# A hybrid layer's MLP on one core: the down projection by Strassen's seven products, interleaved with the next block's up products

## The chip, the core and the metric

The kernel runs on one core of one Trainium2 chip. TensorE (PE) multiplies matrices, VectorE (DVE), ScalarE (ACT) and GpSimd (POOL) work element by element, and SyncE (SP), POOL and others issue DMA transfers. The metric is the device time of one launch in microseconds (us).

## The reference, cut to what matters

One layer is computed for 384 tokens of 2048 features, all in float32: 256 tokens of a new stream ("prompt") and 128 of running streams ("sample"). A mixer comes first (one wide input projection, a pooling branch, a state-space scan, an output projection), then the part that is changed, the MLP:

```
x = x + rmsnorm(m, g_mix_post)
hdn = square(relu(rmsnorm(x, g_mlp_pre) @ w_up)) @ w_down      # 2048 -> 8192 -> 2048
x = x + rmsnorm(hdn, g_mlp_post)
```

## The kernel before, in words

**Three passes for one product.** Every float32 operand of a large product is split in two: `h` is the value rounded to the type fp32r (an ACT copy), `l` the rest (a DVE subtraction). A product is then three matmuls of 128 x 128 by a moving operand: h by h, h by l, l by h, summed in PSUM (`mm3`, L79; `half`, L84, makes 24 of them from half of a weight tile). `wfetch` (L61) has SP load 128 x 1024 weights (512 KB), `wsplit` (L66) splits them. Weights as loaded, `h` and `l` have three buffers each.

**Stages.** Tokens lie in three blocks of 128 (`b` = 0 and 1 prompt, 2 sample). In the input projection (`proj`, L93; 129 tiles of 128 outputs: 16 pool, 16 + 16 gates, 1 dt, 80 for scan and z), in the gate, pool, scan and up projections the weights are the stationary operand and 384 tokens the moving one: one tile of 128 outputs over 2048 inputs is 48 matmuls of 384 columns. The tokens' halves are `xgh`/`xgl` for the input projection, `ah`/`al` (`A`) for the pool projection, `abh`/`abl` for the scan's, `x1h`/`x1l` (`xs2`, L717 to L727) for the up projection. In the output and down projections (`moving`, L641) the tokens are stationary (`mh`/`ml`, `hh`/`hl`) and 512 columns of weights move.

**The MLP** (L730 on) goes over 8 blocks (`c8`) of 1024 of the 8192 hidden features. For each block it makes eight up tiles: 48 matmuls, then DVE's relu with the norm (L763), ACT's square (L764), the split to `hh`/`hl` (L767, L768). Then it takes the down products in four groups of 512 columns (`nb`), each 8 x 3 x 3 = 72 matmuls of 512 columns. `done` (L773) adds them to `hacc` in SBUF on DVE (L778; a copy by ACT in the first block, L776). In the last block each column group is squared, summed and multiplied with `g_mlp_post`, and the last one is followed by the norm (`postnorm`), the residual `x1` and the output. `x1` stays in SBUF throughout.

**Order.** The order on each engine is set by the tile framework's planner from the order of the program, with a few held back by hand (`hold`, `gate`). Tiles lie in pools at addresses that follow from the pools' order and sizes; small `pad` tiles (L212, L634) only move what comes after them.

Of the kernel before, what the change touches and what calls it, by code (L numbers as in the profile page):

```python
# [34 lines left out]
def build(ctx, tc, io):  # L35
# [8 lines left out]

    cst = consts.tile([P, C_END], F32, name="cst")
    vec = consts.tile([P, V_END], F32, name="vec")
# [3 lines left out]
    def mmtile(name):  # L50
        return psm.tile([P, 512], F32, tag="mm", name=name)
# [24 lines left out]
    def wload(src, name):  # L76
        return wsplit(wfetch(src, name))
# [133 lines left out]

    small.tile([P, 24], F32, name="pad_small")  # L212
    tok = small.tile([P, 11, NH], F32, name="tok")
    decb = small.tile([P, NH, NB], F32, name="decb")
    with tc.tile_pool(name="phc", bufs=1, reuse_waits="tile") as pc, tc.tile_pool(name="phc2", bufs=2, reuse_waits="tile") as pc2:
# [10 lines left out]
        def pool_tile(gi, k4):  # L226
# [35 lines left out]
            )  # L262
            rc = cst[:, C_RC + gi * 16 : C_RC + gi * 16 + 16]
            v.tensor_tensor(d[:, :16], cur[:, 15:31], rc, ALU.mult)
# [33 lines left out]
        def dt_phase(pb):  # L298
# [22 lines left out]
            v.tensor_scalar(dta, dt, nA, -1.0, ALU.mult, ALU.mult)  # L321
            v.tensor_tensor_scan(cum, cst[:NH, C_SCAN : C_SCAN + T], dta, 0.0, ALU.mult, ALU.add)
            sy.dma_start(cum_scr, cum)
# [45 lines left out]
    with tc.tile_pool(name="phd", bufs=2, reuse_waits="tile") as pd, tc.tile_pool(  # L369
# [46 lines left out]
        for g in range(G):  # L416
# [27 lines left out]
            for p4 in range(4):  # L444
# [8 lines left out]
                CT[:, TP:].unsqueeze(1).to_broadcast([P, 2, P]),  # L453
                cst[:, C_CM : C_CM + 256].rearrange("p (a t) -> p a t", a=2),
                ALU.mult,
# [6 lines left out]
            cbm = pd.tile([P, 512], F32, tag="cbm", name=f"cbm{g}")  # L462
            v.tensor_tensor(cbm, cb, cst[:, C_MASK : C_MASK + 512], ALU.mult)

# [170 lines left out]

    res = ctx.enter_context(tc.tile_pool(name="res", bufs=1, reuse_waits="tile"))

    x1 = res.tile([P, 3, DM], F32, name="x1")
    r2 = res.tile([P, T], F32, name="r2")

    def moving(o, units, lhs, tail, done):  # L641
# [41 lines left out]
    with tc.tile_pool(name="phf", bufs=1, side="right", reuse_waits="tile") as pf, tc.tile_pool(  # L683
# [19 lines left out]
        for i in range(4):  # L703
# [10 lines left out]
            if i == 0:  # L714
                gate[1] = ins
    pga = ctx.enter_context(tc.tile_pool(name="pga", bufs=1, reuse_waits="tile"))
    xs2 = []  # L717
    for k in range(KD):
# [8 lines left out]
        xs2.append((h, l))  # L727
    mpool.close()

    with tc.tile_pool(name="phg", bufs=1, reuse_waits="tile") as pg, tc.tile_pool(  # L730
        name="phg2", bufs=2, reuse_waits="tile"
    ) as pg2:
        st = pg.tile([P, 3, 4], F32, name="st2")
        for b in range(3):
            for i in range(4):
                q = pg2.tile([P, 512], F32, tag="q3", name=f"q2_{b}_{i}")
                s.activation(q, x1[:, b, blk(i)], AF.Square, accum_out=st[:, b, i : i + 1])
        dg = pg.tile([P, 3, P], F32, name="dg2")
        for b in range(3):
            y = postnorm(pg2, st, b, "n2")  # L740
# [4 lines left out]
        hacc = pg.tile([P, 3, DM], F32, name="hacc")  # L745
        gpo = pg.tile([P, DM], F32, name="gpo2")
        gp.dma_start(gpo, io["g_mlp_post"].partition_broadcast(P))
        st3 = pg.tile([P, 3, 4], F32, name="st3")
        NC = 8
        for c8 in range(NC):  # L750
            hh = []
            for f8 in range(8):
                f = c8 * 8 + f8
                if f == 0:
                    ps = mmtile("pj_up0")[:, :T]
                    half(ps, 0, wload(io["w_up"][0, 0], "up0_0"), xs2)
                    hold[:] = gate
                    half(ps, 1, wload(io["w_up"][0, 1], "up0_1"), xs2)
                else:
                    ps = proj([io["w_up"][f, 0], io["w_up"][f, 1]], xs2, f"up{f}")  # L760
                    hold[:] = [None, None]
                t = pg2.tile([P, T], F32, tag="t", name=f"ht{f}")
                v.scalar_tensor_tensor(out=t, in0=ps, scalar=0.0, in1=r2, op0=ALU.max, op1=ALU.mult)  # L763
                s.activation(t, t, AF.Square)  # L764
                h = pg2.tile([P, T], F32R, tag=f"hh{f8}", name=f"hh{f}", bufs=1)
                l = pg2.tile([P, T], F32R, tag=f"hl{f8}", name=f"hl{f}", bufs=1)
                s.activation(h, t, AF.Copy)  # L767
                v.tensor_tensor(l, t, h.bitcast(F32), ALU.subtract)  # L768
                hh.append((h, l))
            for nb in range(4):  # L770
                o = [mmtile(f"wd{c8}_{nb}_{b}") for b in range(3)]

                def done(b):  # L773
                    dst = hacc[:, b, blk(nb)]
                    if c8 == 0:
                        s.copy(dst, o[b])  # L776
                        return
                    v.tensor_tensor(dst, o[b], dst, ALU.add)  # L778
                    if c8 < NC - 1:
                        return  # L780
                    q = pg2.tile([P, 512], F32, tag="q3", name=f"q3_{nb}_{b}")
                    s.activation(q, dst, AF.Square, accum_out=st3[:, b, nb : nb + 1])
                    v.tensor_tensor(dst, dst, gpo[:, blk(nb)], ALU.mult)
                    if nb < 3:
                        return
                    y = postnorm(pg2, st3, b, "n3")
                    for i in range(4):
                        z = hacc[:, b, blk(i)]
                        xb = x1[:, b, blk(i)]
                        if i >= (0, 2, 3)[b]:  # L790
                            s.activation(z, z, AF.Copy, scale=y)
                            gp.tensor_tensor(z, z, xb, ALU.add)
                        else:
                            v.scalar_tensor_tensor(out=z, in0=z, scalar=y, in1=xb, op0=ALU.mult, op1=ALU.add)
                        sy.dma_start(io["y"][b][:, blk(i)], z)

                moving(
                    o,
                    [(io["w_down"][c8, nb, kp], f"wd{c8}_{nb}_{kp}") for kp in range(4)],
                    hh,  # L800
                    3 if c8 == NC - 1 and nb == 3 else 0,
                    done,
                )


# [30 lines left out]
def _moving(np, w):  # L836
    r, c = w.shape
    return np.ascontiguousarray(w.reshape(r // 256, 2, P, c // 512, 512).transpose(3, 0, 2, 1, 4)).reshape(c // 512, r // 256, P, 1024)


# [79 lines left out]
```

## Time and profile before

| What | us |
|---|---|
| Time of a launch, median of 3 runs (2887.78 to 2889.4) | 2888.16 |
| Span of the profiled execution, first to last instruction | 2886.1 |
| PE busy | 2862.9 (99%) |
| DVE busy | 1548.9 (54%) |
| ACT busy | 1108.4 (38%) |
| POOL busy | 142.4 (5%) |
| Bytes read from and written to HBM | 404.48 and 41.72 MB |

The profile is one execution. Its page gives each engine's busy time, the same in 40 equal slices of the span (a digit is tenths), the DMA queues, the chain of work that ended last followed back from the last instruction, and groups of equal instructions: line, engine, operation, output and inputs, shapes, count, then busy us, mean ns of one, and the idle time before them with what ended it. The trace behind it can be asked for single instructions in order of time: start (us), duration (us), engine, line, operation, tiles. Matmuls overlap one another in these records, so what one costs is read from the distance between starts. Line numbers are those of the kernel before.

### The profile page before, as it was taken

The page shows a single profiled execution, that of the slowest core. Times are in us where ns is not written, and L with a number is a line of the kernel's source. Part 1 is how long each engine was busy: PE and PEld are TensorE (multiplying, and loading weights), DVE is VectorE, ACT ScalarE, POOL GpSimd, SP SyncE. Part 2 cuts the span into 40 slices and gives each one's busy share as a digit, 9 for nine tenths or more (in the row PEclk, how much of TensorE's full clock was granted, in tenths as well). Part 3 has the DMA queues.
Part 4 walks back from the last instruction along what each step waited for, and adds up shares of the span by engine and source line. Part 5 has one row for each costly group of instructions (what it writes and reads, how often), then busy time and mean ns, then how long its engine had stood idle before and what let it go on. Part 6 is the DMA issues. An engine that isn't in the chain of part 4 may idle for free.

```text
span 2886.1 us, 40192 instructions
## 1 busy us (share of the span) xinstructions
PE 2862.9 (99%) x16165; PEld 2702.5 (94%) x16165; DVE 1548.9 (54%) x2306; ACT 1108.4 (38%) x1628; POOL 142.4 (5%) x178
## 2 busy tenths in 40 slices
PE   9999999999999999999999999999999999999998
PEld 8999999999999999999999988989898998989896
DVE  7773335668678678677533334534444444444445
ACT  5343224445445345344422223533232333333233
POOL 0000000011011011011000000000000000000001
PEclk9999999999999999999999999999999999999999
DMA  6444445466456456466744453434443444444443
GB/s 214 132 130 140 137 137 190 149 200 211 160 196 211 151 203 210 146 221 204 224 147 152 146 179 120 130 126 130 126 130 126 130 126 131 125 131 124 131 125 117
DMA packets 141914, 448.82 MB, mean 156 GB/s; under 512 B 17456, under 2 KB 41072, under 8 KB 137120
## 3 DMA queue, kind: packets, MB, share of 16 engines
q1 hardware_dynamic: 133152, 410.14, 44.9%
q0 software_dynamic: 8576, 36.13, 3.3%
q8 instruction: 126, 2.06, 0.3%
q14 instruction: 60, 0.49, 0.1%
HBM read 404.48 MB, written 41.72 MB: 155 GB/s over the span
## 4 chain that ended last, share of the span: by engine, by line
PE 98%; DVE 1%; DMA 0%; ACT 0%; issue 0%; SPq 0%; DVEq 0%; ACTq 0%
PE pj_up L82 6%; PE pj_up L81 6%; PE pj_up L80 6%; PE wd L650 6%; PE wd L649 6%; PE wd L648 6%; PE pj_x L82 5%; PE pj_x L80 5%; PE pj_x L81 5%; PE pj_z L81 3%; PE pj_z L82 3%; PE pj_z L80 3%; PE pj_sp L80 3%; PE pj_sp L82 3%; PE pj_sp L81 3%; PE pj_gb L80 2%
## 5 line engine op out<-in xcount | busy, mean ns | idle before, releaser
L81 PE MATMUL pj_up<-x1l,wh_up 128*128 128x384 f32 x1024 | 343.2, 335 | 0.0
L80 PE MATMUL pj_up<-x1h,wh_up 128*128 128x384 f32 x1024 | 343.1, 335 | 0.0
L82 PE MATMUL pj_up<-x1h,wl_up 128*128 128x384 f32 x1024 | 342.7, 335 | 0.0
L650 PE MATMUL wd<-wh_wd,hl 128*128 128x512 f32 x768 | 298.9, 389 | 0.0
L649 PE MATMUL wd<-wl_wd,hh 128*128 128x512 f32 x768 | 298.9, 389 | 0.0
L648 PE MATMUL wd<-wh_wd,hh 128*128 128x512 f32 x768 | 298.7, 389 | 0.0
L73 DVE TENSOR_TENSOR wl_wd<-w_wd,wh_wd 128x1024 fp32r<-128x1024 f32 x128 | 156.9, 1225 | 263.2 <-ACT wh_wd L71 263.2
L71 ACT ACTIVATE wh_wd<-w_wd 128x1024 fp32r<-128x1024 f32 x128 | 136.1, 1063 | 350.9 <-PE wd L650 284.3
L80 PE MATMUL pj_x<-xgh,wh_x 128*128 128x384 f32 x768 | 264.0, 344 | 0.0
L73 DVE TENSOR_TENSOR wl_up<-w_up,wh_up 128x1024 fp32r<-128x1024 f32 x128 | 156.9, 1226 | 198.1 <-ACT wh_up L71 198.1
L82 PE MATMUL pj_x<-xgh,wl_x 128*128 128x384 f32 x768 | 261.0, 340 | 0.0
L71 ACT ACTIVATE wh_up<-w_up 128x1024 fp32r<-128x1024 f32 x128 | 135.9, 1064 | 325.6 <-PE pj_up L81 264.8
L81 PE MATMUL pj_x<-xgl,wh_x 128*128 128x384 f32 x768 | 259.8, 338 | 0.0
L80 PEld LDWEIGHTS pj_up<-x1h,wh_up 128*128 128x128 f32 x1024 | 192.5, 188 | 0.7 <-ACT x1h L725 0.4
L81 PEld LDWEIGHTS pj_up<-x1l,wh_up 128*128 128x128 f32 x1024 | 192.6, 188 | 0.4
L82 PEld LDWEIGHTS pj_up<-x1h,wl_up 128*128 128x128 f32 x1024 | 192.5, 188 | 0.1
L81 PE MATMUL pj_z<-xgl,wh_z 128*128 128x384 f32 x512 | 173.1, 338 | 0.0
L80 PE MATMUL pj_z<-xgh,wh_z 128*128 128x384 f32 x512 | 172.9, 338 | 0.0
L82 PE MATMUL pj_z<-xgh,wl_z 128*128 128x384 f32 x512 | 172.9, 338 | 0.0
L650 PEld LDWEIGHTS wd<-wh_wd,hl 128*128 128x128 f32 x768 | 144.1, 188 | 30.0
L649 PEld LDWEIGHTS wd<-wl_wd,hh 128*128 128x128 f32 x768 | 144.1, 188 | 29.9
L648 PEld LDWEIGHTS wd<-wh_wd,hh 128*128 128x128 f32 x768 | 144.2, 188 | 29.6
(280 smaller groups left out, 6230.9 us busy)
## 6 DMA issues: line engine op xcount, KB each, us to landing
w_up<-w_up SPq DMA_DIRECT2D x128, 512.0 KB, 3.4
w_wd<-w_down SPq DMA_DIRECT2D x128, 512.0 KB, 3.4
w_x<-w_in SPq DMA_DIRECT2D x96, 512.0 KB, 3.7
w_z<-w_in SPq DMA_DIRECT2D x64, 512.0 KB, 3.5
w_sp<-w_ssd SPq DMA_DIRECT2D x64, 512.0 KB, 3.5
w_ga<-w_in SPq DMA_DIRECT2D x32, 512.0 KB, 3.5
w_pp<-w_pp SPq DMA_DIRECT2D x32, 512.0 KB, 3.5
hs<-ssm SPq DMA_DIRECT2D x16, 1024.0 KB, 6.3
```

Source lines behind the costliest of these rows:

```text
L71: s.activation(h, w, AF.Copy)
L73: v.tensor_tensor(l, w, h.bitcast(F32), ALU.subtract)
L80: te.matmul(out, wh, xh, start=first, stop=False)
L81: te.matmul(out, wh, xl, start=False, stop=False)
L82: return te.matmul(out, wl, xh, start=False, stop=last)
L648: te.matmul(o[b], mh, wh[:, c], start=k == 0, stop=False)
L649: te.matmul(o[b], mh, wl[:, c], start=False, stop=False)
L650: te.matmul(o[b], ml, wh[:, c], start=False, stop=k == nk - 1)
```

## The change

**Seven products.** For the first seven blocks the down product of the 256 prompt tokens is made by the Winograd form of Strassen's scheme. The 1024 features are cut in two halves of 512, 1024 columns at a time (`p` = 0, 1) in two of 512, and the tokens in two of 128. The seven products are made from blocks of tokens, blocks of weights, four sums of token blocks (`token_sums`: five additions and a split, in two calls for each feature block) and four sums of weight blocks (`down_units`: `add`, DVE, 2048 columns each, in place in the loaded weights `raw`). The 128 sample tokens (sums 7 and 8) are multiplied directly with the four unsummed weight blocks. `steps` lists eight weight matrices in order, each with the one or two products that it feeds and the sum that is made after its split. All eight are split, so that a feature block has 32 splits of down weights instead of 16.

**Sums over the blocks in DRAM.** Each of the nine results of a half leaves PSUM by an ACT copy to one of two buffers `ev` and a POOL transfer to `acc_scr`, plain in the first block, accumulating (`accum_op`) in the others. In the last block, whose down product is made as before, the 18 sums are loaded back (`begin_last`), seven of each half are put together by DVE (`merge`), and the last block's products are added.

**Interleaving.** A list of units is worked through by `run` in an order written out (`manual_schedule`): two halves of down weights, one half of an up tile of the next block, and so on. A unit is fetched eight units ahead and split four units ahead, after the matmuls of the unit that held the buffers; every fourth split goes to a fourth pair of buffers (`split4`). The hidden activations have two sets of buffers.

**Room and places.** `x1` goes to DRAM after the output projection and comes back in the last block; `x1h`/`x1l` move to the other side of SBUF, where `mh`/`ml` were. Most of the constants (`cst2`) move to the pool `small`, `pad_small` grows, `pad_m` goes. This moves other tiles too: counted in bytes past a multiple of 512 in the allocation of the built programs, `xgh`/`xgl` go from 128 to 0, `mh`/`ml` from 384 to 480, `x1h`/`x1l` from 0 to 480; the weight buffers and `hh`/`hl` stay at 0, `ah`/`al` at 64.

```diff
-    cst = consts.tile([P, C_END], F32, name="cst")
+    cst = consts.tile([P, 352], F32, name="cst")
...
+    cst2 = small.tile([P, C_END - C_MASK], F32, name="cst2")
...
-    sy.dma_start(cst, io["cst"])
+    sy.dma_start(cst[:, :C_MASK], io["cst"][:, :C_MASK])
+    sy.dma_start(cst2, io["cst"][:, C_MASK:])
...
-    small.tile([P, 24], F32, name="pad_small")
+    small.tile([P, 88], F32, name="pad_small")
...
-        mp.tile([P, 24], F32, name="pad_m")
...
+    x1_scr = dram.tile([P, 3, DM], F32, name="x1_scr")
+    acc_scr = [[dram.tile([P, 512], F32, name=f"acc_scr{p}_{i}") for i in range(9)] for p in range(2)]
...
-    pga = ctx.enter_context(tc.tile_pool(name="pga", bufs=1, reuse_waits="tile"))
+    gp.dma_start(x1_scr, x1)
+    mpool.close()
+    pga_hold = ExitStack()
+    pga = pga_hold.enter_context(tc.tile_pool(name="pga", bufs=1, side="right", reuse_waits="tile"))
...
+    t8 = pg.tile([P, 8, T], F32, name="t8")
+    sf = pg.tile([P, 4, 2, P], F32, name="sf")
+    sh = pg.tile([P, 4, 4, P], F32R, name="sh")
+    sl = pg.tile([P, 4, 4, P], F32R, name="sl")
...
+    DEPTH = 4
+
+    def split4(w, name):
+        turn[0] += 1
+        if turn[0] % DEPTH:
+            return wsplit((w, name))
+        h = pg.tile([P, 1024], F32R, tag="xh", name=f"wh_{name}")
+        l = pg.tile([P, 1024], F32R, tag="xl", name=f"wl_{name}")
+        s.activation(h, w, AF.Copy)
+        v.tensor_tensor(l, w, h.bitcast(F32), ALU.subtract)
+        return h, l
+
+    def run(units, far=8):
+        n = len(units)
+        got, hl = [None] * n, [None] * n
+
+        def fetch(i):
+            if i < n and units[i][0]:
+                got[i] = units[i][0]()
+
+        def prep(i):
+            if i < n:
+                hl[i] = units[i][1](got[i])
+
+        for i in range(far):
+            fetch(i)
+        for i in range(DEPTH):
+            prep(i)
+        for i, (_, _, mm, post, soon) in enumerate(units):
+            fetch(i + far)
+            mm(hl[i])
+            if soon:
+                post()
+            prep(i + DEPTH)
+            if not soon:
+                post()
+            hl[i] = got[i] = None
+
+    nothing = lambda *_: None
+
+    def token_sums(k):
+        a11, a12 = t8[:, k, :P], t8[:, 4 + k.start : 4 + k.stop, :P]
+        a21, a22 = t8[:, k, P:TP], t8[:, 4 + k.start : 4 + k.stop, P:TP]
+        f = [sf[:, i, :, :] for i in range(4)]
+        v.tensor_tensor(f[0], a22, a21, ALU.subtract)
+        v.tensor_tensor(f[3], a11, a12, ALU.subtract)
+        v.tensor_tensor(f[3], f[3], f[0], ALU.add)
+        v.tensor_tensor(f[2], a11, a21, ALU.subtract)
+        v.scalar_tensor_tensor(out=f[1], in0=f[0], scalar=-1.0, in1=a11, op0=ALU.mult, op1=ALU.subtract)
+        s.activation(sh[:, :, k, :], sf, AF.Copy)
+        v.tensor_tensor(sl[:, :, k, :], sf, sh[:, :, k, :].bitcast(F32), ALU.subtract)
+
+    def up_evict(f, ps):
+        f8 = f % 8
+        t = t8[:, f8, :]
+        v.scalar_tensor_tensor(out=t, in0=ps, scalar=0.0, in1=r2, op0=ALU.max, op1=ALU.mult)
+        s.activation(t, t, AF.Square)
+        blocks = range(3) if f8 >= 4 else (0, 2)
+        n = len(blocks)
+        tag = f"{f8}_{f // 8 % 2}"
+        h = pg.tile([P, n, P], F32R, tag=f"hh{tag}", name=f"hh{f}")
+        l = pg.tile([P, n, P], F32R, tag=f"hl{tag}", name=f"hl{f}")
+        tb = t.rearrange("p (b t) -> p b t", b=3)
+        if n == 2:
+            tb = tb[:, 0:3:2, :]
+        s.activation(h, tb, AF.Copy)
+        v.tensor_tensor(l, tb, h.bitcast(F32), ALU.subtract)
+        return {b: (h[:, i, :], l[:, i, :]) for i, b in enumerate(blocks)}
+
...
+    NAMES = ("11", "12", "22", "21")
+
+    def down_units(c8, p, hh):
+        nm = f"{c8}_{p}"
+        tok = lambda k0, b: lambda k: hh[k0 + k][b]
+        sums = lambda i: lambda k: [sh[:, i, k, :], sl[:, i, k, :]]
+        raw, t2 = {}, []
+        src = {n: io["w_down"][c8, p, i] for i, n in enumerate(NAMES)}
+
+        def add(d, n):
+            v.tensor_tensor(raw[d], raw[d], raw[n], ALU.add)
+
+        steps = [
+            ("11", True, [(0, tok(0, 0)), (7, tok(0, 2))], nothing),
+            ("12", True, [(8, tok(0, 2))], lambda: add("11", "12")),
+            ("21", True, [(1, tok(4, 0)), (7, tok(4, 2))], nothing),
+            ("22", True, [(2, sums(3)), (8, tok(4, 2))], lambda: add("12", "22")),
+            ("11", False, [(4, sums(0))], lambda: add("22", "11")),
+            ("12", False, [(6, sums(2))], lambda: add("21", "22")),
+            ("22", False, [(5, sums(1))], nothing),
+            ("21", False, [(3, tok(4, 1))], nothing),
+        ]
+        begins, ends = {7: 0, 8: 1}, {7: 2, 8: 3}
+
+        def evict(r, o):
+            e = pg.tile([P, 512], F32, tag="ev", name=f"ev{nm}_{r}", bufs=2)
+            s.copy(e, o)
+            if c8 == 0:
+                gp.dma_start(acc_scr[p][r], e)
+            else:
+                gp.dma_start(acc_scr[p][r], e, accum_op=ALU.add)
+
+        out = []
+        for j, (kd, load, uses, then) in enumerate(steps):
+            outs = []
+            for q in range(2):
+                half_cols = slice(q * 1024, q * 1024 + 1024)
+
+                def fetch(kd=kd, q=q, hc=half_cols):
+                    if q == 0:
+                        raw[kd] = pr.tile([P, 2048], F32, tag="raw", name=f"raw{nm}_{kd}")
+                    sy.dma_start(raw[kd][:, hc], src[kd][:, hc])
+
+                def prep(_, j=j, q=q, kd=kd, hc=half_cols, then=then):
+                    hl = split4(raw[kd][:, hc], f"wd{nm}_{j}_{q}")
+                    if q:
+                        then()
+                    return hl
+
+                def mm(hl, j=j, q=q, uses=uses, outs=outs):
+                    if j == 0 and q == 0:
+                        t2.extend(sstile(f"t2_{nm}_{i}") for i in range(2))
+                    if q == 0:
+                        outs += [t2[r - 7] if r >= 7 else mmtile(f"wd{nm}_{r}") for r, _ in uses]
+                    wh, wl = hl
+                    for k2 in range(2):
+                        k = q * 2 + k2
+                        c = slice(k2 * 512, k2 * 512 + 512)
+                        for (r, a), o in zip(uses, outs):
+                            ah, al = a(k)
+                            first = k == 0 and (r < 7 or begins[r] == j)
+                            fin = k == 3 and (r < 7 or ends[r] == j)
+                            te.matmul(o, ah, wh[:, c], start=first, stop=False)
+                            te.matmul(o, ah, wl[:, c], start=False, stop=False)
+                            te.matmul(o, al, wh[:, c], start=False, stop=fin)
+
+                def post(j=j, q=q, uses=uses, outs=outs):
+                    if q == 0:
+                        return
+                    for (r, _), o in zip(uses, outs):
+                        if r < 7 or ends[r] == j:
+                            evict(r, o)
+                    if p == 0 and j < 2:
+                        token_sums(slice(2 * j, 2 * j + 2))
+
+                out.append((fetch if load else None, prep, mm, post, False))
+        return out
+
...
+    def begin_last():
+        raws.close()
+        fin = ctx.enter_context(tc.tile_pool(name="fin", bufs=1, reuse_waits="tile"))
+        for p in range(2):
+            ac.append([fin.tile([P, 512], F32, name=f"ac{p}_{i}") for i in range(9)])
+            for i in range(9):
+                gp.dma_start(ac[p][i], acc_scr[p][i])
+
...
+    def enter_last():
+        pga_hold.close()
+        begin_last()
...
+        gp.dma_start(tail["gpo"], io["g_mlp_post"].partition_broadcast(P))
+        gp.dma_start(tail["x1"], x1_scr)
...
+    for i in range(NC - 1):
+        down = down_units(i, 0, hs_[i]) + down_units(i, 1, hs_[i])
+        ups = up_units(i + 1, hs_[i + 1])
+        for j in range(16):
+            units += down[2 * j : 2 * j + 2] + ups[j : j + 1]
+    last = last_units(hs_[c8])
...
+    with tc.manual_schedule():
+        run(units)
```

More of the change, by code (lines that the diff above doesn't have):

```diff
@@ L744, in build @@
         s.copy(r2, bc[:, :T])
[L745 to L758, printed above, removed]
-                else:
[L760 to L776, printed above, removed]
-                        return
[L778 to L802, printed above, removed]
-                )
@@ new lines, in up_units, with mm, post @@
+    def up_units(c8, hh, skip=0):
+        out = []
+        for f8 in range(skip, 8):
+            f = c8 * 8 + f8
+            ps = []
+            for q in range(2):
+                def mm(hl, f=f, q=q, ps=ps):
+                    if q == 0:
+                        ps.append(mmtile(f"pj_up{f}")[:, :T])
+                    half(ps[0], q, hl, xs2)
+                def post(f=f, f8=f8, q=q, ps=ps):
+                    if q:
+                        hh.append(up_evict(f, ps[0]))
+                out.append(
+                    (lambda f=f, q=q: wfetch(io["w_up"][f, q], f"up{f}_{q}"), lambda w: split4(*w), mm, post, True)
+                )
+        return out
@@ new lines, in last_done @@
+    def last_done(nb, bs, o):
+        lp2, st3, gpo = tail["lp2"], tail["st3"], tail["gpo"]
+        for b in bs:
+            v.tensor_tensor(hacc[b][nb], o[b], hacc[b][nb], ALU.add)
+        for b in bs:
+            q = lp2.tile([P, 512], F32, tag="q3", name=f"q3_{nb}_{b}")
+            s.activation(q, hacc[b][nb], AF.Square, accum_out=st3[:, b, nb : nb + 1])
+        for b in bs:
+            v.tensor_tensor(hacc[b][nb], hacc[b][nb], gpo[:, blk(nb)], ALU.mult)
+        if nb < 3:
+            return
+        for b in bs:
+            y = postnorm(lp2, st3, b, "n3")
+            for i in range(4):
+                z = hacc[b][i]
+                xb = tail["x1"][:, b, blk(i)]
+                if i >= (0, 2, 3)[b]:
+                    s.activation(z, z, AF.Copy, scale=y)
+                    gp.tensor_tensor(z, z, xb, ALU.add)
+                else:
+                    v.scalar_tensor_tensor(out=z, in0=z, scalar=y, in1=xb, op0=ALU.mult, op1=ALU.add)
+                sy.dma_start(io["y"][b][:, blk(i)], z)
@@ new lines, in build @@
+    hh0 = []
+    ps = mmtile("pj_up0")[:, :T]
+    half(ps, 0, wload(io["w_up"][0, 0], "up0_0"), xs2)
+    hold[:] = gate
+    half(ps, 1, wload(io["w_up"][0, 1], "up0_1"), xs2)
+    hold[:] = [None, None]
+    hh0.append(up_evict(0, ps))
+    hs_ = [hh0] + [[] for _ in range(NC - 1)]
+    units = up_units(0, hs_[0], 1)
+    for i in range(NC - 1):
[3 more added lines that the diff above has]
+            units += down[2 * j : 2 * j + 2] + ups[j : j + 1]
@@ L877 @@
         "w_up": _tiles(np, a["w_up"][0], range(0, 4 * DM, P)),
[L878 to L880 removed]
+        "w_down": _paired(np, a["w_down"][0][: 7 * 1024]),
+        "w_dlast": _moving(np, a["w_down"][0][7 * 1024 :]),
         "state_pool": np.ascontiguousarray(a["state_pool"][0].reshape(NB, 15, KD, P).transpose(3, 2, 0, 1)),
```

111 lines of the change are left out of this document (95 added, 16 removed).

## The prediction

> **What bounds the kernel now.** I read the page's head and chain first (which engine is the bound), then starts of single matmuls (what one costs, stage by stage), then the groups by line and the transfers (whether the other engines can carry the new work).
>
> ```profile
> span 2886.1 us, 40192 instructions
> PE 2862.9 (99%) x16165; PEld 2702.5 (94%) x16165; DVE 1548.9 (54%) x2306; ACT 1108.4 (38%) x1628; POOL 142.4 (5%) x178
> ...
> DVE  7773335668678678677533334534444444444445
> ...
> PEclk9999999999999999999999999999999999999999
> ...
> GB/s 214 132 130 140 137 137 190 149 200 211 160 196 211 151 203 210 146 221 204 224 147 152 146 179 120 130 126 130 126 130 126 130 126 131 125 131 124 131 125 117
> ...
> PE 98%; DVE 1%; DMA 0%; ACT 0%; issue 0%; SPq 0%; DVEq 0%; ACTq 0%
> ```
>
> PE is 98% of the chain that ends last, at full clock in every slice: time is number of matmuls times the step from one to the next. That step is not the "mean ns" of a group, since matmuls overlap; it is read from starts. In the MLP, by order of time:
>
> ```profile
> 1948.86 0.33 PE L80 MATMUL pj_up<-x1h,wh_up 128*128 128x384 f32 x1
> ...
> 2015.44 0.39 PE L648 MATMUL wd<-wh_wd,hh 128*128 128x512 f32 x1
> ...
> 2080.76 0.33 PE L80 MATMUL pj_up<-x1h,wh_up 128*128 128x384 f32 x1
> ```
>
> One block of 1024 features is 384 up matmuls in 66.58 us (173.4 ns each) and 288 down matmuls in 65.32 us (226.8 ns each), without a gap.
>
> The span is one profiled execution; the median of the runs, 2888.16, stands 2.1 above it, and I carry that over: forecast = 2888.2 plus the sum.
>
> **Part 1, fewer matmuls.** For each of seven blocks and each 1024 columns, the seven products of 256 prompt tokens need 7 x 4 x 3 = 84 matmuls and the 128 sample tokens 2 x 8 x 3 = 48: 132 in place of 144. Over 14 such pairs that is 168 matmuls fewer, which is also the difference of the two PE instruction lists. They are of the same form, with operands that both start at multiples of 512 bytes as before: 168 x 0.2268 = **-38.1 us**, all on the path.
>
> **Part 2, where the operands lie.** In the allocation of the built programs, counted in bytes past a multiple of 512, the weight buffers are at 0 in both kernels. The layer's input xgh/xgl goes from 128 to 0, mh/ml of the output projection from 384 to 480, x1h/x1l of the up projection from 0 to 480; ah/al stay at 64. Does it matter? The gate and pool projections alternate, same lines, same shapes:
>
> ```profile
> 299.72 0.34 PE L80 MATMUL pj_pp<-ah,wh_pp 128*128 128x384 f32 x1
> ...
> 308.04 0.33 PE L80 MATMUL pj_ga<-xgh,wh_ga 128*128 128x384 f32 x1
> ...
> 316.47 0.34 PE L80 MATMUL pj_pp<-ah,wh_pp 128*128 128x384 f32 x1
> ...
> 324.79 0.33 PE L80 MATMUL pj_ga<-xgh,wh_ga 128*128 128x384 f32 x1
> ...
> L648 PE MATMUL wo<-wh_wo,mh x192: 390/393/404, 1669.5 to 1802.6; 128*128 128x512 f32 x192
> ```
>
> 48 matmuls on ah (at 64) take 8.32 us, both times; 48 on xgh (at 128) take 8.43; 48 up matmuls (at 0) took 66.58/8 = 8.32. The output projection steps (1802.6 - 1669.5)/573 = 232.3 ns, the down projection 226.8, at the same width: the first has its operands 384 bytes apart, the second 0. So distances 0 and 64 go with the short step, 128 and 384 with the long. The 129 projections of the layer's input lie at distance 0 afterwards: 129 x 0.11 = **-14.2 us**. The instruction order up to the MLP is otherwise the same, row for row. The output projection's weights lie 32 bytes beyond its tokens afterwards, between the two fast distances: 576 x 5.5 ns = **-3.2 us** (0 if not). The up projection's moving operand gets 480, that is 32 short of 512; nothing in the trace has that distance. The nearest row is distance 0, so I take no cost; like distance 128 it would be 64 x 0.11 = +7.0 us.
>
> [...]
>
> **Part 3, the new work of DVE and ACT beside PE.**
>
> ```profile
> 1948.90:2080.80 131.90, 131.90 (x674) 120.63 (x673) 54.79 (x59) 42.11 (x50) 0.00 (x0) 1.00 0.42 128
> ...
> L73 DVE TENSOR_TENSOR wl_wd<-w_wd,wh_wd 128x1024 fp32r<-128x1024 f32 x128 | 156.9, 1225 | 263.2 <-ACT wh_wd L71 263.2
> L71 ACT ACTIVATE wh_wd<-w_wd 128x1024 fp32r<-128x1024 f32 x128 | 136.1, 1063 | 350.9 <-PE wd L650 284.3 <-PE pj_up L81 66.5
> L778 DVE TENSOR_TENSOR hacc<-wd,hacc 128x512 f32<-128x512 f32 x84 | 57.5, 692 | 13.5 <-PE wd L650 13.5
> L768 DVE TENSOR_TENSOR hl<-ht,hh 128x384 fp32r<-128x384 f32 x64 | 35.4, 552 | 1.2 <-ACT hh L767 1.2
> L767 ACT ACTIVATE hh<-ht 128x384 fp32r<-128x384 f32 x64 | 33.8, 528 | 2.0
> L764 ACT ACTIVATE ht<-ht 128x384 f32<-128x384 f32 x64 | 32.5, 508 | 0.6 <-DVE ht L763 0.6
> L776 ACT COPY hacc<-wd 128x512 f32<-128x512 f32 x12 | 7.0, 587 | 7.4 <-PE wd L650 6.6
> L252 DVE SCALAR_TENSOR_TENSOR d<-win,pbuf 128x256 f32<-128x256 f32 x16 | 6.8, 426 | 0.3
> ...
> L573 DVE TENSOR_TENSOR hs<-hs,decb x16: 2282/2284/2286, 552.9 to 1334.3; 128x2048 f32<-128x2048 f32 x16
> ...
> L763 DVE SCALAR_TENSOR_TENSOR ht<-pj_up,r x64: 557/558/559, 1830.9 to 2807.1; 128x384 f32<-128x384 f32 x64
> ```
>
> The first row is a stage of one block: us, then busy time of PE, PEld, DVE (54.79), ACT (42.11), POOL, clock, DMA share, GB/s; in the last two, least, median and longest ns, first and last start. Afterwards a block has PE for 384 x 0.1734 + 264 x 0.2268 = 126.5 us. DVE has 48 splits instead of 32 (eight weight matrices are used, four of them sums), 48 x 1.225 = 58.8; eight sums of 2048 columns, 8 x 2.284 = 18.3; two token sums, 2 x (5 x 0.426 + 1.225) = 6.7; eight evictions of up tiles, at most 8 x (0.558 + 0.552) = 8.9. That is 92.7. The order is now written out, so DVE also stands still for ACT between the two halves of an eviction, 8 x (0.508 + 0.528) = 8.3, and in the token sums, 2 x 1.063: together 103, 81% of 126.5. ACT: 48 x 1.063 + 18 x 0.587 + 8.3 + 2.1 = 72, 57%. Neither is the bound over a block.
>
> The tight place is steps 3 to 5 of the eight, whose preparation carries a sum each. Two halves of weights and half an up tile give PE 12 x 0.2268 + 24 x 0.1734 = 6.9 us where a step feeds one product; DVE needs 3 x 1.225 + 2.284 + half of 2.1 = 7.0. Preparation runs four units ahead, and during it PE is still in steps 2 and 3, which feed two products and last 9.6 us; and three prepared units (6.9 us at least) stand against one split chain of 1.06 + 1.23. So I take **0**. If the cover fails for one sum in each block it is 7 x 2.28 = +16 us. Late next would be ACT's copy out of the two PSUM sums, queued behind the splits.
>
> **Part 4, the running sums in DRAM.**
>
> ```profile
> w_wd<-w_down SPq DMA_DIRECT2D x128, 512.0 KB, 3.4
> new_ssm_s<-hs POOLq DMA_DIRECT2D x16, 1024.0 KB, 4.8
> a_scr<-zs POOLq DMA_DIRECT2D x32, 192.0 KB, 2.4
> gpo<-g_mix_post SPq DMA_DIRECT2D x4, 256.0 KB, 3.6
> y<-hacc SPq DMA_DIRECT2D x12, 256.0 KB, 2.1
> ...
> L588 POOL DMA_DIRECT2D new_ssm_s<-hs x16: 539/548/559, 570.8 to 1352.8; - x16
> ```
>
> 72 of the 84 additions of hacc on DVE go, and 14 merging ones of that length come in the last block, where DVE has room; 18 products a block leave by an ACT copy and a POOL transfer of 256 KB, accumulating from the second block on. No row has an accumulating transfer. Bounds: 2.1 us (a 256 KB store) and 3.6 + 2.1 = 5.7 (a load, then a store); I take 5.7, since it must read what it adds to. There are two buffers for the copies, and the closest pair that share one is 6.9 us apart, so ACT does not wait: 0. Behind a waiting copy stand the next splits on ACT, then DVE, then PE. Traffic: 16.8 MB of weights and 4.7 MB read and written in 126.5 us are 207 GB/s; slices before reached 224.
>
> [...]
>
> In the last block, nine sums for each half come back (18 x 256 KB), then g (1 MB), then x1 (3 MB), on POOL's queue. When the first 512 columns are done, DVE waits for g, and behind it stands the split of unit 8, which PE needs 8 x 18 x 0.2268 = 32.7 us into the block. These 5.8 MB and four units of weights (2.1 MB) ahead of it need 35 us at 224 GB/s, 27 us at the rate by which the stores of 1024 and 256 KB differ (768 KB in 2.7 us). After g there are three products of 0.69 and a split, 3.3 us. Cost 0 to 35 + 3.3 - 32.7 = 6; nearer the second rate, since DVE's wait holds the weights back, I take **+2**. The 3 MB store of x1, three times 4.8 us, lies between the last output matmuls (1802.6) and the first write into its room (L763, 1830.9): 0.
>
> **Sum:** -38.1 - 14.2 - 3.2 + 2 = -53.5, so **2835 us**; its own range 2829 to 2849 (up: +7.0 for x1h, +4 for the last block, +3.2 for the output projection; down: the 2 of the last block, 1.3 for 129 tiles read to 0.01 us, the 2.1 around the span).
>
> **Rivals.** *Distance does nothing* (the long step belongs to xgh and mh for another reason): 2888.2 - 38.1 + 2 = 2852. For: no rule known here; against: the alternating pair. 0.15. *DVE becomes the bound in the tight steps*: +16 us by one sum a block, 2851, up to +35 us, half of 18 x 0.55 us of POOL's issuing a block if that blocks DVE, 2870. For: 7.0 against 6.9 us. Against: in the scan, among POOL's stores, all 16 products of 2048 columns took 2282 to 2286 ns. 0.20. *Accumulating transfers are slow*, the slower side: nine copies a half-block share two buffers, so a half-block of 63.2 us can't be shorter than 4.5 x (landing + 0.6). From a landing of 13.4 us on this binds, and each us more costs 14 x 4.5 = 63 us; at 14.3 the gain is gone, at 15 it is 2835 + 101 = 2936. Against: 5.7 us. 0.13. *The saved matmuls come back as waits of equal length*, within 0.2%: 0.04.
>
> **How the numbers follow.** The forecast has 0.48. Faster: 0.48 + 0.15 + 0.20 = 0.83; within 0.2% (5.8 us, about what a measurement tells): 0.04; slower: 0.13. The range goes from the forecast's lower end to the DVE rival's upper, 2829 to 2870, leaving out the slow transfers and little else.
>
> **What would show it.** Part 1: 168 matmuls fewer and some 126.5 us a block. Part 2: 48 matmuls on xgh in 8.32 us, wo at 226.8 ns, pj_up still at 173.4. Part 3: DVE near 0.73 busy, sums near 2284 ns, PE without gaps. Part 4: landings of acc_scr under 6.9 us, no ACT copy waiting for DMA. Wrong if PE shows idle time behind DVE or ACT in the seven blocks, or if pj_x keeps 8.43 us.

## The result, and the profile after

| | before | after |
|---|---|---|
| Time of a launch, median of 4 runs, us | 2888.44 (2887.78 to 2889.4) | 2840.61 (2840.38 to 2840.92) |
| Span of the profiled execution, us | 2886.1 | 2838.9 |
| Start of the last matmul in it, us | 2871.98 | 2820.76 |

The ratio is 0.9834 with an interval of 0.982 to 0.9848: 47.8 us faster, where 53.5 were forecast. The page of the changed kernel begins:

```profile
span 2838.9 us, 40540 instructions
...
PE 2811.2 (99%) x15997; PEld 2655.9 (94%) x15997; DVE 1798.0 (63%) x2501; ACT 1280.2 (45%) x1869; POOL 254.8 (9%) x324
...
PEclk9999999999999999999999999999999999999999
...
PE 97%; DVE 1%; ACT 0%; issue 0%; DVEq 0%; ACTq 0%
```

PE is still the chain that ends last, now with 15997 matmuls: 168 fewer. Two blocks of the MLP, then the last one (us, then busy time of PE, PEld, DVE, ACT, POOL, clock, DMA share, GB/s):

```profile
1930.00:2056.50 126.50, 126.50 (x650) 116.18 (x649) 88.60 (x85) 67.25 (x85) 12.27 (x18) 1.00 0.55 169
2056.50:2183.00 126.50, 126.50 (x650) 116.18 (x649) 88.57 (x85) 67.25 (x85) 15.45 (x18) 1.00 0.64 171
2753.00:2821.00 68.00, 68.00 (x305) 56.58 (x303) 42.23 (x61) 25.73 (x44) 14.76 (x24) 1.00 0.62 237
```

PE has no gap in any of them, DVE is busy for 88.6 of 126.5 us (92.7 were counted; in the records each piece overlaps the next by some 0.1 us) and ACT for 67.3 (72). Starts of single matmuls of the gate and pool projections (in order of time), and then what the trace answers for four lines and the landing of L882 (durations in ns: least, median, longest; first and last start; the last row, from the page, holds all transfers to acc_scr):

```profile
305.47 0.34 PE L80 MATMUL pj_ga<-xgh,wh_ga 128*128 128x384 f32 x1
313.81 0.33 PE L80 MATMUL pj_pp<-ah,wh_pp 128*128 128x384 f32 x1
322.13 0.34 PE L80 MATMUL pj_ga<-xgh,wh_ga 128*128 128x384 f32 x1
```

```profile
L652 PE MATMUL wo<-wh_wo,mh x192: 393/396/398, 1655.5 to 1789.2; 128*128 128x512 f32 x192
L862 DVE TENSOR_TENSOR raw<-raw,raw x56: 2282/2284/2289, 1875.3 to 2733.3; 128x2048 f32<-128x2048 f32 x56
L880 POOL DMA_DIRECT2D acc_scr<-ev x18: 539/539/544, 1877.6 to 1994.5; - x18
L882 POOL DMA_DIRECT2D acc_scr<-ev x108: 842/855/1229, 2004.1 to 2754.4; - x108
DMA to landing us min/median/max: 3.8/4.9/8.8
acc_scr<-ev POOLq DMA_DIRECT2D x126, 256.0 KB, 4.6
```

The 48 matmuls on xgh now take 8.34 us, those on ah 8.32 as before. The output projection steps at (1789.2 - 1655.5)/573 = 233.3 ns; before it was 232.3. The sums take 2284 ns. An accumulating transfer (L882) lands in 4.9 us and holds POOL for 0.86, where a plain one of the same size (L880) holds it for 0.54.

The end after the last matmul is where time was given back. Before, from its start at 2871.98 to the end of the span 14.1 us pass; afterwards 18.1. Four rows of that stretch before, in order of time: four products of POOL, the last matmul, a product of DVE of one element a partition, and the three steps of DVE that write the last results:

```profile
2870.72 6.30 POOL L792 TENSOR_TENSOR hacc<-hacc,x 128x512 f32<-128x512 f32 x4
...
2871.98 0.39 PE L650 MATMUL wd<-wh_wd,hl 128*128 128x512 f32 x1
2872.04 0.44 DVE L677 TENSOR_TENSOR n_n<-n_n,n_n 128x1 f32<-128x1 f32 x1
...
2878.90 3.08 DVE L794 SCALAR_TENSOR_TENSOR hacc<-hacc,n_n,x 128x512 f32<-128x512 f32 x3
```

and the same stretch of the changed kernel, in the same order of time:

```profile
2820.35 2.93 POOL L981 TENSOR_TENSOR ac<-ac,x1b 128x512 f32<-128x512 f32 x2
...
2820.76 0.39 PE L999 MATMUL wd<-wh_wd,hl 128*128 128x512 f32 x1
2820.86 1.22 DVE L673 TENSOR_TENSOR n_n<-st 128x1 f32<-128x1 f32 x1
2822.11 1.18 DVE L674 TENSOR_TENSOR n_n<-n_n,st 128x1 f32<-128x1 f32 x1
...
2827.60 1.50 DVE L971 TENSOR_TENSOR ac<-ac,gpo 128x512 f32<-128x512 f32 x1 [0.79 <-ACT q L969]
2829.02 0.15 DVE L673 TENSOR_TENSOR n_n<-st 128x1 f32<-128x1 f32 x1
...
2830.86 3.08 DVE L983 SCALAR_TENSOR_TENSOR ac<-ac,n_n,x1b 128x512 f32<-128x512 f32 x3
```

DVE reaches the last three steps 6.9 us after the last matmul's start before and 10.1 afterwards. The partial sums of the norm over the first three column groups (L673, L674) now stand behind the fourth group's product, as the order is written out; the planner of the kernel before had put them earlier. They are additions of one element a partition, yet take 1.2 us each while POOL works; the same addition for the next block of tokens, at 2829.02, when POOL stood idle, takes 0.15.

### The profile page after: what moved, and what is told of

The parts are those of the page before. It is cut to its first block, busy times and chain, and to the rows that moved or that the text cites. A ratio compares the mean times of both kernels' runs of the same rounds, so it can differ in the third digit from the quotient of the medians.

```text
span 2838.9 us, 40540 instructions
## 1 busy us (share of the span) xinstructions
PE 2811.2 (99%) x15997; PEld 2655.9 (94%) x15997; DVE 1798.0 (63%) x2501; ACT 1280.2 (45%) x1869; POOL 254.8 (9%) x324
## 3 DMA queue, kind: packets, MB, share of 16 engines
HBM read 412.34 MB, written 77.89 MB: 173 GB/s over the span
## 4 chain that ended last, share of the span: by engine, by line
PE 97%; DVE 1%; ACT 0%; issue 0%; DVEq 0%; ACTq 0%
PE pj_up L80 6%; PE pj_up L81 6%; PE pj_up L82 6%; PE pj_x L82 5%; PE pj_x L80 5%; PE pj_x L81 5%; PE wd L914 3%; PE pj_sp L80 3%; PE wd L916 3%; PE wd L915 3%; PE pj_z L82 3%; PE pj_z L80 3%; PE pj_sp L81 3%; PE pj_z L81 3%; PE pj_sp L82 3%; PE t L914 2%
## 5 line engine op out<-in xcount | busy, mean ns | idle before, releaser
L73 DVE TENSOR_TENSOR wl_wd<-raw,wh_wd 128x1024 fp32r<-128x1024 f32 x168 | 202.3, 1222 | 68.8 <-ACT wh_wd L71 66.9
L71 ACT ACTIVATE wh_wd<-raw 128x1024 fp32r<-128x1024 f32 x168 | 175.1, 1054 | 96.9 <-PE pj_up L81 84.2
L82 PE MATMUL pj_sp<-abh,wl_sp 128*128 128x384 f32 x512 | 171.0, 334 | 0.0
L80 PE MATMUL pj_sp<-abh,wh_sp 128*128 128x384 f32 x512 | 171.0, 334 | 0.0
L81 PE MATMUL pj_sp<-abl,wh_sp 128*128 128x384 f32 x512 | 171.0, 334 | 0.0
L73 DVE TENSOR_TENSOR wl_sp<-w_sp,wh_sp 128x1024 fp32r<-128x1024 f32 x64 | 78.3, 1224 | 118.9 <-ACT wh_sp L71 118.1
L882 POOL DMA_DIRECT2D acc_scr<-ev x108 | 92.7, 928 | 667.5 <-ACT ev L878 650.6
L80 PEld LDWEIGHTS pj_x<-xgh,wh_x 128*128 128x128 f32 x768 | 144.3, 188 | 2.5 <-issue 1.4
L82 PEld LDWEIGHTS pj_x<-xgh,wl_x 128*128 128x128 f32 x768 | 144.2, 188 | 2.6 <-issue 2.6
L81 PEld LDWEIGHTS pj_x<-xgl,wh_x 128*128 128x128 f32 x768 | 144.3, 188 | 1.1 <-issue 0.2
```

What stands on the lines that cost most here:

```text
L71: s.activation(h, w, AF.Copy)
L73: v.tensor_tensor(l, w, h.bitcast(F32), ALU.subtract)
L80: te.matmul(out, wh, xh, start=first, stop=False)
L81: te.matmul(out, wh, xl, start=False, stop=False)
L82: return te.matmul(out, wl, xh, start=False, stop=last)
L882: gp.dma_start(acc_scr[p][r], e, accum_op=ALU.add)
```

## The experiments

Two questions stood behind the numbers: whether the distance between the two operands of a matmul really sets its step, and how much room DVE and the transfers had left. A third came from the result: what the tail and the output projection cost.

### Part 2 alone, and everything but it

The first run does to the kernel before what the change does to the input projection's operand, and nothing else:

```diff
-    small.tile([P, 24], F32, name="pad_small")
+    small.tile([P, 56], F32, name="pad_small")
```

> The kernel before with one edit: 32 more floats of padding in the pool small, which moves xgh/xgl of the input projection from 128 to 0 bytes past a multiple of 512, where the weights lie, and nothing else. Distance theory: the 129 input tiles lose 0.11 us each, so 48 matmuls on xgh take 8.32 us as on ah, and the time is 2888.4 - 13.4 to 14.2, about 2874.5. Rival (distance does nothing, xgh had the long step for another reason): 2888 and 8.43 us as before.

Measured: 2874.22 us (2873.13 to 2874.37), 14.4 less than the 2888.63 of the kernel before beside it, ratio 0.995 (0.9934 to 0.9967). The second run takes this part out of the changed kernel:

```diff
-    small.tile([P, 88], F32, name="pad_small")
+    small.tile([P, 56], F32, name="pad_small")
```

> The changed kernel with one edit: 32 floats of padding fewer, which puts xgh/xgl back at 128 bytes from the weights; everything else as changed. Distance theory: +13.4 to +14.2, so about 2854.5, with 8.43 us for 48 matmuls on xgh; what is left against the kernel before is then part 1 and the tail, about -34. Rival: 2840.6, no difference.

Measured: 2855.02 us (2854.75 to 2856.39), 14.4 more than the changed kernel. So this part is worth 14.4 us in either direction, and the rival "distance does nothing" falls. What is left for all other parts is 2888.63 - 2855.02 = 33.6 us.

### Distance, or the place of one operand?

Both runs move the tokens; it could be their own place that counts. The next run starts from the second one and moves the weights instead, by the same 128 bytes:

```diff
     cst = consts.tile([P, 352], F32, name="cst")
+    consts.tile([P, 32], F32, name="pad_c")
```

> The run xg_back with one more edit: 32 floats of padding ahead of the weight buffers, so that the weights and all that lies on that side go from 0 to 128 bytes past a multiple of 512, while xgh/xgl stay where they were in xg_back, at 128. If the distance between the two operands decides, xgh is at distance 0 again and 48 matmuls take 8.32 us (173.3 ns each); if the place of the moving operand itself decides, they keep xg_back's 8.44 us (175.9). The output projection's weights get 160 past mh, x1h 352 past the weights: two more points of the map.

The run with xgh at 128 and weights at 0, starts of single matmuls:

```profile
307.98 0.33 PE L80 MATMUL pj_ga<-xgh,wh_ga 128*128 128x384 f32 x1
316.42 0.34 PE L80 MATMUL pj_pp<-ah,wh_pp 128*128 128x384 f32 x1
```

and with both at 128:

```profile
304.79 0.34 PE L81 MATMUL pj_ga<-xgh,wh_ga 128*128 128x384 f32 x1
313.13 0.33 PE L81 MATMUL pj_pp<-ah,wh_pp 128*128 128x384 f32 x1
```

8.44 us become 8.34, with xgh at the same addresses. The distance decides, not the place. (The run's 2854.04, a single time, is no measure of that: x1h came to 352 bytes from the weights, and the up projection's step rose to 176.7 ns.)

### A map of distances

Three runs move five operands each by padding in their pools. Their times (2883.0, 2862.51 and 2892.59 us, a single time each) aren't read, since in them PE also waited for abh at the start of the scan's projection (9.1 us in the first); the padding beside abh is the likely reason, not a shown one. Their steps are read stage by stage. The first run's edit:

```diff
-    small.tile([P, 88], F32, name="pad_small")
+    small.tile([P, 80], F32, name="pad_small")
...
+        pc.tile([P, 8], F32, name="pad_a")
...
+        pe1.tile([P, 40], F32, name="pad_ab")
...
+        mp.tile([P, 112], F32, name="pad_m")
...
+    pga.tile([P, 56], F32, name="pad_g")
```

The pads stand ahead of ah/al and abh/abl, and behind mh/ml and x1h/x1l. In this order of lines the second run has 96, 32, 56, 56 and 40 floats, the third 0, 56, 96, 8 and 16.

> The changed kernel with five operands moved by padding, each read in its own stage by the distance between starts: xgh at 32, ah at 96, abh at 160, x1h at 256 bytes past the weights, and the output projection's weights 480 past mh. If the cost depends on distance modulo 512 and is smooth, as the prediction took it, 32, 96 and 480 have the short step (173.3 ns at 384 columns, 226.8 ns at 512 columns) and 160 and 256 the long one (175.9 ns). If it depends on a coarser rule (multiples of 64 short, or multiples of 128 long), 256 and 32 tell it. If distance does nothing, every stage keeps the steps of the changed kernel and the time is 2840.6.

> As the run before, with other distances: xgh at 480, ah at 192, abh at 224, x1h at 320 bytes past the weights, and the output projection's weights 256 past mh. A smooth dependence: 480 short (173.3 ns), 192, 224 and 320 long (175.9 ns), 256 at 512 columns long (232 ns). No dependence: all stages as in the changed kernel.

> Five more points of the map, read from the steps: xgh at 352, ah at 288, abh at 384, x1h at 416 bytes past the weights, the output projection's weights 64 past mh. If the cost is symmetric about distance 0, 352 (as 160), 384 (as 128) and 416 (as 96) have the long step of 176 to 177 ns, and 288 (as 224) the short one of 173.3; 352 was long in the run shift at another stage. If it isn't symmetric, 384 or 416 are short. 64 at 512 columns: short (226.8) if the two widths follow one map, long (232 to 234) if 32 and 160 on both sides decide.

The output projection in these three runs, in this order, then in the run with shifted weights (least, median and longest duration, first and last start; 573 steps lie between):

```profile
L655 PE MATMUL wo<-wh_wo,mh x192: 392/396/396, 1691.1 to 1824.8; 128*128 128x512 f32 x192
```

```profile
L655 PE MATMUL wo<-wh_wo,mh x192: 389/389/391, 1679.3 to 1809.2; 128*128 128x512 f32 x192
```

```profile
L655 PE MATMUL wo<-wh_wo,mh x192: 393/394/394, 1703.1 to 1834.2; 128*128 128x512 f32 x192
```

```profile
L653 PE MATMUL wo<-wh_wo,mh x192: 392/397/400, 1654.8 to 1789.0; 128*128 128x512 f32 x192
```

133.7, 129.9, 131.1 and 134.2 us. The pool projection's 48 matmuls, ah at 96 (first run) and at 192 (second):

```profile
317.21 0.34 PE L80 MATMUL pj_pp<-ah,wh_pp 128*128 128x384 f32 x1
325.68 0.34 PE L80 MATMUL pj_ga<-xgh,wh_ga 128*128 128x384 f32 x1
```

```profile
315.53 0.34 PE L80 MATMUL pj_pp<-ah,wh_pp 128*128 128x384 f32 x1
323.85 0.34 PE L80 MATMUL pj_ga<-xgh,wh_ga 128*128 128x384 f32 x1
```

8.47 and 8.32 us. All stages together, bytes from the stationary to the moving operand modulo 512 (counted so, the output projection of the kernel before lies at 128, where the prediction counted the other way and said 384), and ns from start to start once a run of equal matmuls has settled:

| moving columns | short | long | in between |
|---|---|---|---|
| 384 (173.3 short) | 0, 64, 192, 224, 320, 416, 480 | 96, 128, 160, 288, 352, 384 (176 to 177) | 32 (173.3 in some tiles, 176.7 in others); 256 (173.3, but some six longer steps behind each change to it) |
| 512 (226.7 short) | 0, 256 | 32, 128, 160, 480 (232 to 234) | 64 (228.9) |

The distance matters by 1.5% to 3%, but not smoothly: 32, which I expected short, is in between at one width and long at the other, and 192, 224 and 320 are short. Nor is it symmetric about 0: 96 is long and 416 short, 224 short and 288 long. Of the seven distances read at both widths, only 0 is short in every stage. The two widths also differ in which operand moves, the tokens or the weights, so that the width itself is not shown to make the difference. Why the distance matters stays open; the map is one of measurements, without a rule.

In the interleaved MLP the place of the up projection's operand shows in the down matmuls behind it as well, though their own operands lie at distance 0. With x1h at 352 the first nine of twelve down matmuls behind each half of an up tile took about 231 ns, and the down projection of the last block alone stayed at 226.7. It is not only the long step that does this: with x1h at 256 and at 416, where the up projection itself settles at 173.3 ns, the first nine took 231 ns too, with x1h at 320 the first three, and at 480 all stayed at 227. So a distance that the table calls short can still cost something behind a change of operands.

### The two missed terms, and a version with both mended

First the output projection's operand to 0:

```diff
             ms_.append((h, l))
+        mp.tile([P, 120], F32, name="pad_m")
```

> The changed kernel with one edit: 120 floats of padding after mh/ml, which puts them at 0 instead of 480. Distance theory: the output projection steps at 226.8 ns instead of 233.3, 576 x 6.5 ns = -3.7 us, about 2836.9; that is the -3.2 that the prediction counted and that did not come. Rival (the output projection steps at 232 to 233 ns for another reason, its stationary tokens for one): 2840.6.

```profile
L653 PE MATMUL wo<-wh_wo,mh x192: 387/389/390, 1655.8 to 1785.7; 128*128 128x512 f32 x192
```

(1785.7 - 1655.8)/573 = 226.7 ns, -3.8 us in the stage; the launch takes 2837.51 us (2836.66 to 2837.88), 3.1 less. Then the norm's partial sums:

```diff
+        if nb == 2:
+            tail["pre"] = [presum(lp2, st3, b, "n3") for b in range(3)]
         if nb < 3:
             return
         for b in bs:
-            y = postnorm(lp2, st3, b, "n3")
+            y = postnorm(lp2, st3, b, "n3", tail["pre"][b])
```

`presum` is the first three lines of `postnorm`: the two additions, the scaling and the offset.

> The changed kernel with one edit: the partial sums of the last norm over the first three column groups, with their scaling and offset, are made by DVE after the third group instead of after the last matmul. If the order written out for DVE costs the tail its 4.0 us, the time from the last matmul to the end goes from 18.1 to about 14.1 us and the launch to 2836.6 to 2837.5. Rival (the tail is longer because of POOL's four products, the later load of x1 or the stores): at most 1 us, 2839.6 to 2840.6.

```profile
2819.12 6.30 POOL L988 TENSOR_TENSOR ac<-ac,x1b 128x512 f32<-128x512 f32 x4
...
2820.37 0.39 PE L1006 MATMUL wd<-wh_wd,hl 128*128 128x512 f32 x1
...
2827.30 3.08 DVE L990 SCALAR_TENSOR_TENSOR ac<-ac,n_n,x1b 128x512 f32<-128x512 f32 x3
```

DVE's last steps start 6.9 us after the last matmul's start, as in the kernel before, and the launch takes 2837.25 us (2837.07 to 2837.64), 3.4 less. The span ends at 2835.3, 14.9 us after that start: 0.8 of the 4.0 remain, between DVE's last steps and the end of the stores, and weren't followed. Both edits together:

> The two edits of mh0 and presum together. If both mechanisms hold they add up, as they lie in different stages: 2840.6 - 3.7 - 3.5 = 2833.4. If only one holds, 2837; if neither, 2840.6.

2834.44 us (2833.69 to 2834.83), ratio to the kernel before 0.9814 (0.98 to 0.9827). It is 6.2 us faster than the changed kernel and the fastest here; the two gains add up.

### How much room DVE had

```diff
             v.tensor_tensor(raw[d], raw[d], raw[n], ALU.add)
+            v.tensor_tensor(raw[d], raw[d], raw[d], ALU.max)
```

> The changed kernel with each of the 56 sums of weight blocks followed by a second pass of DVE over its 2048 columns that changes no value (the maximum of the sum with itself). DVE's work in a block goes from 88.6 to about 107 of 126.5 us; in steps 3 to 5 of the eight, DVE needs 7.0 + 2.28 = 9.3 us against PE's 6.9. If the four prepared units cover it, as the prediction took it, at most some us are lost: 2841 to 2850. If the tight steps bind (rival: DVE becomes the bound there), each of 14 half-blocks loses up to 3 x 2.4 = 7.2 us: up to 2941, with PE idle behind the splits. In between, the reserve is used up step by step: 2850 to 2900.

Measured: 2911.85 us (2910.3 to 2913.4), 71.2 more than the changed kernel: the rival's mechanism, at seven tenths of its upper price. PE's waits from the first MLP block on are these two groups (sum, times, longest):

```profile
PE pj_up L82 <- DVE wl_up L771: 35.9, 14, 3.3
PE pj_up L82 <- DVE wl_up L73: 11.9, 14, 1.0
```

The changed kernel has none there. Its reserve can be read from its own trace, in the split that follows the third sum of a half-block and the first matmul that uses it:

```profile
1976.46 1.22 DVE L771 TENSOR_TENSOR wl_up<-w_up,wh_up 128x1024 fp32r<-128x1024 f32 x1
```

```profile
1979.08 0.34 PE L82 MATMUL pj_up<-x1h,wl_up 128*128 128x384 f32 x1
```

The split is ready at 1977.68, 1.4 us before PE needs it: that is the smallest distance of a split to its use in the seven blocks, and it comes back in each half-block, at 1.4 to 1.5. Three passes more are 6.9 us; less 1.4 that is 5.5, and the three steps of a first half-block are indeed late by 1.1, 0.9 and 3.5 us. By this reserve, as an estimate, a single pass more (2.28 us) ahead of that split would already have made PE wait; no run here tries it.

Idle PE can cost twice. Four stretches of the same run (us, PE busy, clock, DMA share, GB/s): a wait of 3.6 us from one start to the next, of which PE stood idle for 3.3; what follows it; and what follows each of two waits of 2.2 us, 1.8 of them idle:

```profile
1919.70:1923.30 3.60, 0.35 (x2) 0.90 0.18 74
1923.30:1929.30 6.00, 5.94 (x19) 0.50 0.80 253
...
1991.60:1997.00 5.40, 5.40 (x29) 1.00 0.81 266
2127.50:2130.70 3.20, 3.20 (x11) 0.50 0.92 237
```

After this wait of 3.6 us PE runs 6 us at half the granted clock. After the wait of 2.2 us that ended at 1991.5 it keeps the full clock; after an equal one that ended at 2126.2 it loses half of it 1.2 us later (last row). Neither length decides it: of the seven waits of 3.6 us in the run, one for each block, five come with the half clock (for 6.8 us three times, for 3.4 us twice) and two do not; of the seven of 2.2 us, two do (for 3.4 us) and five do not. Summed over the starts, waits take 52 us and slow steps 18 of the 72.7 by which the two spans differ.

### Accumulating against plain transfers

```diff
-                gp.dma_start(acc_scr[p][r], e, accum_op=ALU.add)
+                gp.dma_start(acc_scr[p][r], e)
```

> The changed kernel with all 18 transfers of a block as plain stores instead of accumulating ones: it leaves out the addition over the blocks, so the down product holds only the seventh and the eighth block. If the accumulating transfers are hidden, as the prediction took it, the time is 2840.6 within 1 us, and only their landing (4.6 us) and their issue on POOL (0.93 us) get shorter. Rival (accumulating costs the path, by DVE's waiting for POOL's issue or by DMA traffic that the weights need): 2 to 35 us faster.

```profile
L882 POOL DMA_DIRECT2D acc_scr<-ev x108: 542/542/551, 2003.1 to 2752.7; - x108
...
acc_scr<-ev POOLq DMA_DIRECT2D x126, 256.0 KB, 2.5
```

2840.94 us (2840.53 to 2841.35): no difference. Accumulating nearly doubles the landing (2.5 to 4.6 us by the medians over all 126) and lengthens POOL's part by 0.3 us, all of it hidden.

## Why the prediction was right, and which terms were not

The time, 2840.6, lies inside the forecast's own range of 2829 to 2849; the mechanism was the forecast's, and three terms were off.

- **Part 1, -38.1: right.** The down matmuls take 331.8 + 152.3 us from start to start (wd and t) instead of 522.3, -38.2, and a block takes 126.50 us.
- **Part 2, input projection, -14.2: right.** -14.4 in both single runs, and 128 against 0 bytes was the cause, by the run that shifts the weights.
- **Part 2, output projection, -3.2: wrong.** "The output projection's weights lie 32 bytes beyond its tokens afterwards, between the two fast distances" is the step that failed: it supposed that what lies between two fast distances is fast, and carried it from 384 columns to 512. The stage gained nothing (233.3 against 232.3 ns, +0.6 us). The note "0 if not" came within 0.6 us of it. With the operand at 0 the stage takes 3.8 us less.
- **Part 2, up projection, 0 with +7.0 as its bound: right, by luck.** 480 is short at 384 columns: 173.5 ns a step, +0.4 us over 3072. But the reason given, a fast neighbour, is of the kind that failed for the output projection, and 480 itself is long at 512 columns.
- **Part 3, 0: right, with less room than told.** No PE wait, sums of 2284 ns. The argument "three prepared units stand against one split chain" held; the reserve was 1.4 us in each half-block, less than one of the 2.28 us sums whose failure I had priced at 16 us. The rival at 0.20 was close by: a second pass behind each sum cost 71.2 us.
- **Part 4: right.** Landing 4.9 us against 5.7 taken and 6.9 allowed. Single ones took up to 8.8, over the 6.9, and still no copy of ACT to `ev` waited for a transfer. The traffic counted, 207 GB/s, stands against 169 to 171 in the blocks shown: HBM reads rose by 7.9 MB in all, to 412.34, which the 18 loads and `x1` make up, so whatever an accumulating transfer reads is not in these counts.
- **The last block, +2: too much.** DVE did wait 3.9 us for `g_mlp_post`, as the prediction had it, but PE, with four units prepared, had no gap in 68.00 us.
- **The tail, not in the sum: missed, +4.0.** I had followed the order up to the last matmul only. The order written out put the norm's two additions and the scaling behind the last product, which the planner had done before; the run that moves them back returns 3.4.

Together -38.2 - 14.4 + 0.6 + 0.4 + 4.0 = -47.6, against -47.8 measured. The forecast stood 5.7 us too low: the output projection and the tail missed by 3.8 and 4.0, and the 2 us too many for the last block hid part of it.

## What to carry to other kernels

Where PE is the bound and matmuls follow without a gap, read the step from starts for each stage, and move both operands to the same offset modulo 512 bytes where two stages of equal shape differ; of the distances tried at both widths only equal offsets were fast in every stage here (173.3 and 226.7 ns), so do not interpolate. When an order is written out by hand, follow it to the very end of the launch: small operations that a planner had slipped into idle time land on the path behind the last matmul (3.4 us here). Before adding work to an engine with much idle time, measure the smallest distance from its result to its use, not its busy share: DVE was 70% busy and had 1.4 us.

## What was not expected of the hardware

- The step of a matmul depends on the distance of its operands, counted here modulo 512 bytes, in no order for which I found a rule: 226.7 ns at 0 and 256, 228.9 at 64, 232 to 234 at 32, 128, 160 and 480 (512 columns). The effect outlasts the operand: behind an up projection at 256, 352 or 416 the next nine matmuls, at distance 0 themselves, took about 231 ns instead of 226.7.
- DVE additions of one element a partition took 1.22 and 1.18 us beside POOL's two-input products, 0.15 without them, and a product of 512 columns 1.50 instead of 0.69; another such product, started at 2820.24 beside them, kept its 0.69. Both additions end within 0.02 us of the end of one of POOL's products (2822.06 and 2823.27). In the kernel before, a DVE product of two such inputs took 0.44 us beside POOL instead of 0.16, while operations with one tensor input, in the same stretch, kept their 0.15 to 0.27. Why they take longer stays open.
- The granted clock fell to a half 1.2 us after a PE gap of 2.2 us (from start to start) ended, and not after five others of the same length; with gaps of 3.6 us it fell five times of seven.
